# Long-convolution filters: plain float32 products in the taps' transform, without the split into high and low parts

## The chip, the cores and the metric

The kernel runs on one core of one Trainium2 chip. The metric is device time in microseconds (us) of one execution. Three runs of the kernel before took 3436.69, 3432.41 and 3435.01 us, median 3435.01 us. The engines are named as the profile names them: PE is TensorE's matmul side and PEld its weight load, DVE is VectorE, ACT is ScalarE, POOL is GpSimd, SP issues the DMAs.

## The reference, cut to what matters

The program is two blocks of a network on 512 tokens of 1024 channels (batch 1), with a context of 256 tokens beside them in the second block. The change lies in one function of the second block, the implicit filters of its long convolutions, which are computed once for n = 256 (context) and once for n = 512 (tokens):

```python
def hyena_filter_freqs(n, w1, b1, w2, b2, w3, freq):
    ...
    hid = jnp.sin(freq[0] * (z @ w1.astype(f32) + b1.astype(f32)))
    hid = jnp.sin(freq[1] * (hid @ w2.astype(f32) + b2.astype(f32)))
    h = (hid @ w3.astype(f32)).reshape(n, 2, HYENA_ORDER, D_B)
    deltas = jnp.abs(jnp.linspace(MIN_DECAY, MAX_DECAY, D_B, dtype=f32))
    h = h * jnp.exp(-t[:, :, None, None] * deltas)
    h_circ = jnp.concatenate(
        [h[:, 0], jnp.zeros((1, HYENA_ORDER, D_B), f32), h[:0:-1, 1]], axis=0)
    h_circ = h_circ / jnp.sum(jnp.abs(h_circ), axis=0, keepdims=True)
    return jnp.fft.rfft(h_circ, axis=0)
```

A small network of sines gives the taps h of two halves (forward and backward in time), two orders and 1024 channels; they are windowed, normalised by the sum of their magnitudes, and transformed over time. Everything is float32.

## The kernel before, in words

Most products of the kernel are made from split operands: `split` (L106) writes H, the operand in 12 significant bits, on ACT (L110), and L, what is left, on DVE (L113); `mm3` (L140) then adds three products, H.H, H.L and L.H (L144 to L146), in a PSUM bank. A few products are made with plain float32 operands and no split, among them the context's own long convolution (L1306, L1333); L1306 makes 32 products of 128 by 128 by 256 (two orders, four channel groups, two frequency tiles, two halves).

The filters come from `hyena_filter` (L1082), one generator for n = 256 and one for n = 512. Its three parts:

- `features` (L1102): the two sine layers, into HL.
- `matrices` (L1130): two constant matrices, cosine and sine, [time, frequency]; they are loaded in pieces and split into H and L by `split` (six pieces over both lengths).
- `groups` (L1208): eight groups of 256 channels. `taps(g)` (L1144) makes for each time tile of 128 (nt = 2 or 4 tiles) a bank with two products (L1160, L1161), the windowed taps `sd` on DVE (L1164; 512 columns, the sum of the two halves beside their difference), a correction of row 0 in the first tile (L1168, L1169), the magnitudes on ACT (L1172) and their sums (L1174, L1177 on DVE, L1178 on POOL), and then the split of `sd`: H on ACT (L1180), L in two halves (L1183), one on DVE and one on POOL. `transform(g, SD, i, nm)` (L1193) makes for each frequency tile (hk = 1 or 2) one bank with the products of the even times in columns 0 to 255 and of the odd times in 256 to 511, each by `mm3`; ACT copies the whole bank to `ae` (L1202), DVE adds its halves (L1204), POOL subtracts them (L1205), and SP sends the result to DRAM (L1206).

Over both lengths there are 48 time tiles, 48 transform banks and 160 products of 128 by 128 by 256, which are 480 matmuls as `mm3` makes them. The bank tag `h_pt` has two buffers, `h_ps` two, `h_sd` two, the split taps four each of H and L, `h_ae` two, `h_hg` three.

`second_block` runs the filters in turns with `gmlp` of the context (first half of its mixer), a step of each at a time. [...] What comes after the filters is the norm of the 512 tokens, and `hyena` of the context in turns with `gmlp` of the tokens; these use the SBUF and the PSUM banks that the filters' pools give back.

Of the kernel before, what the change touches and what calls it, by code (L numbers as in the profile page):

```python
# [17 lines left out]
ALU = mybir.AluOpType  # L18
# [11 lines left out]
class Ctx:  # L30
    """The program's pools and constants."""
# [26 lines left out]
class Scope:  # L58
    """Pools that live for some of the program."""
# [46 lines left out]
def split(k, H, L, src, act=True):  # L106
    """H = src in 12 significant bits, L = what is left."""
    nc = k.nc
    if act:
        nc.scalar.activation(out=H, in_=src, func=AF.Copy)  # L110
    else:
        nc.vector.tensor_copy(out=H, in_=src)
    nc.vector.tensor_tensor(out=L, in0=src, in1=f(H), op=ALU.subtract)  # L113


def wload(k, ap, n, nk, raws=None):
    """ap: DRAM [128, nk*n] -> list over k of (H, L) access patterns [128, n]; raws: the words, if they are loaded."""
    nc = k.nc
    per = max(1, 1024 // n)
    out = []  # L120
    for k0 in range(0, nk, per):
        kk = min(per, nk - k0)
        if raws:
            raw = raws[k0 // per]
        else:
            raw = k.raw.tile([P, kk * n], F32, tag="raw", name="raw", bufs=k.raw_bufs)
            nc.sync.dma_start(out=raw, in_=ap[:, k0 * n:(k0 + kk) * n])
        H = k.wsp.tile([P, kk * n], F32R, tag="wh", name="wh", bufs=k.w_bufs)
        L = k.wsp.tile([P, kk * n], F32R, tag="wl", name="wl", bufs=k.w_bufs)
        split(k, H, L, raw)  # L130
        for t in range(kk):
            out.append((H[:, t * n:(t + 1) * n], L[:, t * n:(t + 1) * n]))
    return out
# [6 lines left out]
def mm3(k, out, terms):  # L140
    """out = sum over terms of (sh+sl).T @ (mh+ml), but for sl.T @ ml, which lies below float32's last bit."""
    n = len(terms)
    for i, ((sh, sl), (mh, ml)) in enumerate(terms):
        k.nc.tensor.matmul(out=out, lhsT=sh, rhs=mh, start=(i == 0), stop=False)  # L144
        k.nc.tensor.matmul(out=out, lhsT=sh, rhs=ml, start=False, stop=False)  # L145
        k.nc.tensor.matmul(out=out, lhsT=sl, rhs=mh, start=False, stop=(i == n - 1))  # L146


class Tr:
    """A transposed activation, [channel, token], in pieces of some channel tiles, high and low parts."""  # L150
# [19 lines left out]
def power(k, ss, w, mult, add, tag="st"):  # L170
    """(ss*mult + add) ** -0.5"""
    nc = k.nc
    a = st(k, w, tag)
    nc.vector.tensor_scalar(out=a, in0=ss, scalar1=mult, scalar2=add, op0=ALU.mult, op1=ALU.add)  # L174
    r = st(k, w, tag)
    nc.gpsimd.tensor_tensor(out=r, in0=a, in1=k.neghalf[:, 0:w], op=ALU.pow)  # L176
    return r


def row_rstd(k, xm, j):  # L180
    """1 / rms of each row; j is room for the squares."""
    ss = st(k, 1)
    k.nc.scalar.activation(out=j, in_=xm, func=AF.Square, accum_out=ss)
    return power(k, ss, 1, 1.0 / 1024, EPS)


def norm_T(k, xm, g, T, m, b=None):
    """rms norm of the token tile xm [128, 1024], times g, plus b (both [128, 8], by channel), into T at tokens m."""
# [38 lines left out]
def tok_mm(k, T, m, w, off=0, ks=None):  # L227
    """The token tile m of T.T @ W in a bank."""
# [6 lines left out]
def add_out(*a, **kw):  # L235
    """x += gate * (T.T @ W), W in column groups of 512."""
    for _ in add_out_steps(*a, **kw):
        pass


def add_out_steps(k, W, T, nk=8, x=None, nt=4, gate=None, after=None, order=None, off=0, lag=2):
    """add_out, a step at a time."""
# [24 lines left out]
def turns(*gens):  # L267
    """Steps of several generators in turn; a pair (generator, n) takes n steps at a time."""
# [14 lines left out]
class Late(list):  # L283
    """Work that waits for other engines, put off by a step."""
# [7 lines left out]
def grp(w, cols):  # L292
    """[K, N] -> [128, (K/128) * len(cols)], the columns of one group, tile by tile of K."""
# [129 lines left out]
def hyena_consts(n, A):  # L423
    """Constants of a sequence length: positional features, decay windows, and the transforms."""
# [33 lines left out]
def a_tables(k, j):  # L458
    """Rotation tables with the gains folded in: [128, 4 token tiles, (q, k), 64]."""
# [18 lines left out]
def a_lambda(k, j, lam_init):  # L478
    """-(exp(q1.k1) - exp(q2.k2) + lambda_init) on every partition, [128, 1]."""
# [13 lines left out]
def layer_a(k, j, lam_init, T, after, w0=None):  # L493
# [51 lines left out]
    def attn(u, i):  # L545
        """A step for each head; the products that wait for a step's other engines come a step later."""
# [80 lines left out]
def layer_b(k, T, after, side):  # L627
    """side: a generator of other work, whose 96 steps are spread over the layer."""
# [24 lines left out]
    def conv(cs, us):  # L653
        """The sums of the taps of two channel tiles, in turn."""
# [20 lines left out]
    def turn(cs, accs):  # L675
        """The sums to token order."""
# [69 lines left out]
def layer_c(k, T, after):  # L746
# [25 lines left out]
    def rope(out, x, t, m, nh):  # L772
        """out = rotated x, both [128, nh, 64]; the gain is in the tables."""
# [120 lines left out]
    def attn(u, i):  # L894
        """A step for each head; the products that wait for a step's other engines come a step later."""
# [73 lines left out]
def mod_setup(k, pool):  # L969
    """silu of both conditions as 32 stationary columns, of which two are used: [128, 8, 32]."""  # L970
# [13 lines left out]
def mod_layers(k, pool, psum, raw_bufs):  # L984
    """The modulation vectors of both layers as columns, [128, 48 (section, channel tile), (c, c_ctx)], in 96 steps."""
# [36 lines left out]
def mod_affine(k, pool, l, which, s, tag):  # L1022
    """Gain and shift by channel of modulate(): g*(1+scale) [128, 8] and shift."""
# [9 lines left out]
def mod_gate(k, pool, l, which, s, tag):  # L1033
    """The gate as a row on every partition, [128, 1024]."""
# [12 lines left out]
def once(make):  # L1047
    """make(), at the first call."""
# [13 lines left out]
def sine(k, out, arg, t):  # L1062
    """out = sin(arg), by way of the remainder of arg by 2 pi; arg is destroyed, t is room."""
# [9 lines left out]
def hyena_filters(k, ns, pool, psum, out):  # L1073
    """The filters of several lengths, a step at a time."""
# [7 lines left out]
def hyena_filter(k, n, pool, psum, out, j):  # L1082
    """The spectra of both orders to DRAM, as (Hr, G) by order and channel group, and 1/(sum|h| 2n) by channel, into
    out[n]; three parts, a step at a time each. The filters' halves are held as their sum and difference, the larger
    magnitude of which is the sum of the halves' magnitudes."""
# [16 lines left out]
    def features():  # L1102
# [12 lines left out]
        h = room("h_sd", 2)[:, 0:n]  # L1115
# [8 lines left out]
        h = room("h_sd", 2)[:, 0:n]  # L1124
# [5 lines left out]
    def matrices():  # L1130
        for nm in ("c", "s"):
            H = pool.tile([P, nt, n // 2], F32R, tag=f"h_m{nm}h{n}", name="h_mh")
            L = pool.tile([P, nt, n // 2], F32R, tag=f"h_m{nm}l{n}", name="h_ml")
            mats[nm] = (H, L)
            for t in range(0, nt, 2):
                raw = room("h_raw", 2)[:, 0:n].rearrange("p (a b) -> p a b", a=2)
                nc.sync.dma_start(out=raw, in_=A[f"h_m{nm}_{n}"][:, t:t + 2])
                split(k, H[:, t:t + 2], L[:, t:t + 2], raw)
            yield
# [4 lines left out]
    def taps(g):  # L1144
        """The windowed sums and differences of a group of 256 channels, [time, channel], by time tile."""
# [11 lines left out]
        SD = [[], []]  # L1157
        for t in range(nt):
# [3 lines left out]
            sd = room("h_sd", 2)  # L1162
# [16 lines left out]
            H, L = (pool.tile([P, 512], F32R, tag=f"h_sd{c}", name="h_hl", bufs=4) for c in "hl")  # L1179
            nc.scalar.activation(out=H, in_=sd, func=AF.Copy)  # L1180
            for i, eng in enumerate((nc.vector, nc.gpsimd)):
                sl = slice(256 * i, 256 * i + 256)
                eng.tensor_tensor(out=L[:, sl], in0=sd[:, sl], in1=f(H[:, sl]), op=ALU.subtract)  # L1183
                SD[i].append((H[:, sl], L[:, sl]))
# [8 lines left out]
    def transform(g, SD, i, nm):  # L1193
        MH, ML = mats[nm]
        for kt in range(hk):
            p = bank("h_pt")
            sl = slice(kt * P, (kt + 1) * P)
            for par in range(2):
                mm3(k, p[:, 256 * par:256 * par + 256],
                    [((MH[:, t, sl], ML[:, t, sl]), SD[i][t]) for t in range(par * nt // 2, (par + 1) * nt // 2)])  # L1200
            ae = room("h_ae", 2)
            nc.scalar.activation(out=ae, in_=p, func=AF.Copy)  # L1202
            hg = pool.tile([P, 2, 256], F32, tag="h_hg", name="h_hg", bufs=3)
            nc.vector.tensor_tensor(out=hg[:, 0], in0=ae[:, 0:256], in1=ae[:, 256:512], op=ALU.add)  # L1204
            nc.gpsimd.tensor_tensor(out=hg[:, 1], in0=ae[:, 0:256], in1=ae[:, 256:512], op=ALU.subtract)  # L1205
# [20 lines left out]
def hyena_tables(k, n, pool, exact):  # L1226
    """The half-sample transforms, forward [t, k] and back [k, t], of both symmetries."""
# [21 lines left out]
def conv_input(k, pool, psum, n, spec, o, cg, z, exact):  # L1249
    """The spectrum of the filter, and z's halves folded and turned to [time, channel]."""  # L1250
# [32 lines left out]
def long_conv(k, pool, psum, n, tabs, D, o, cg, z, ready, exact, skip, out, then=None):  # L1283
    """z (*) filter + skip z, by channel tile; z and the result, out: lists of two [128 channels, n] each; ready: of
    conv_input; then: to be done when that has been used. A step at a time."""
# [72 lines left out]
class Stream:  # L1358
    """A sequence of the second block: n tokens, the residual xs, the transposed input T and the gate row."""
# [11 lines left out]
def gmlp(k, S, G, psum):  # L1371
    """xs += gate * (first half of the mixer), a step at a time."""
# [53 lines left out]
def hyena(k, S, pool, psum, spec, D, exact, after=None):  # L1426
    """xs += gate * (second half of the mixer), a step at a time."""
# [56 lines left out]
def ffn(k, l, streams):  # L1484
    """streams: (T, n, xs, gate, after) each; xs += gate() * swiglu(T)."""
# [34 lines left out]
def layer_attn(k, T, Tc, gate, after, opool):  # L1520
# [89 lines left out]
    def attn(g, i):  # L1610
        """The products that wait for a head's other engines come a head later."""
# [236 lines left out]
```

## Time and profile before

| | us |
|---|---|
| median of three runs | 3435.01 |
| lowest and highest | 3432.41, 3436.69 |
| span of the profiled execution, first to last instruction | 3436.0 |
| PE busy over the span | 3187.3 (93%) |
| DVE busy over the span | 2062.6 (60%) |
| POOL busy over the span | 868.9 (25%) |

For the profiled execution the page gives the span and no other time. Busy time of PE is modelled: matmuls are pipelined, so that one which starts behind another shows a longer duration than the distance to the next start. Stretches are given in us from the span's start; the filters lie between about 1344 and 1588.

### The profile page before, as it was taken

To read this page: it belongs to the slowest core of one execution; us is meant where nothing else is said; L and a number is where in the kernel's file an instruction comes from. 1 tells how busy PE (TensorE), PEld (TensorE's weight loads), DVE (VectorE), ACT (ScalarE), POOL (GpSimd) and SP (SyncE) were. 2 spreads that over 40 slices of the span, in tenths; PEclk is the share of its full clock that TensorE was granted. 3 is DMA by queue.
4 is the path that set the end of the run, shared out by engine and by line. 5 is a ranking of instruction groups with operands and counts; after the bars stand their busy time and mean duration, and the time that the engine had idled before them with its cause. 6 is when DMAs were issued, how large, how long until landed. Compare 5 with 4: busy or idle time off the path is not lost.

```text
span 3436.0 us, 43198 instructions
## 1 busy us (share of the span) xinstructions
PE 3187.3 (93%) x16196; PEld 2499.9 (73%) x16196; DVE 2062.6 (60%) x3794; ACT 1311.9 (38%) x2532; POOL 868.9 (25%) x790
## 2 busy tenths in 40 slices
PE   8999987889999999789999899799999999989998
PEld 6666533478676667668887788588888877778887
DVE  5665799555655666898667677733333265544334
ACT  5444534344444445555333333421222243442222
POOL 1110466101111111784433234212211120012111
PEclk9999998999999999799999999899999999999999
DMA  3112565521021114454333422111112110022222
GB/s 124 50 50 72 192 191 183 191 73 60 28 74 62 62 50 131 146 157 140 121 122 118 125 84 89 53 62 62 62 63 72 63 56 25 25 80 92 95 96 86
DMA packets 109073, 316.35 MB, mean 92 GB/s; under 512 B 11774, under 2 KB 29727, under 8 KB 108864
## 3 DMA queue, kind: packets, MB, share of 16 engines
q1 hardware_dynamic: 108432, 313.17, 28.5%
q8 instruction: 127, 2.08, 0.3%
q14 instruction: 82, 0.67, 0.1%
q10 hardware_dynamic: 432, 0.43, 0.0%
HBM read 297.83 MB, written 15.73 MB: 91 GB/s over the span
## 4 chain that ended last, share of the span: by engine, by line
PE 64%; DVE 18%; ACT 5%; POOL 5%; issue 4%; DMA 3%; POOLq 0%; DVEq 0%; ACTq 0%; SPq 0%
PE mm L144 16%; PE mm L146 16%; PE mm L145 16%; DVE b_a L665 4%; DVE wl L113 3%; PE sc L591 2%; POOL st L176 2%; PE sc L1655 1%; PE fc L144 1%; PE fc L145 1%; PE fc L146 1%; ACT wh L110 1%; PE o L1630 1%; PE o L558 1%; PE pq L1333 1%
## 5 line engine op out<-in xcount | busy, mean ns | idle before, releaser
L113 DVE TENSOR_TENSOR wl<-raw,wh 128x1024 fp32r<-128x1024 f32 (+2 forms) x400 | 506.7, 1270 | 338.5 <-ACT wh L110 333.6
L110 ACT ACTIVATE wh<-raw 128x1024 fp32r<-128x1024 f32 (+2 forms) x400 | 420.4, 1054 | 583.8 <-PE mm L146 303.3
L144 PE MATMUL mm<-wh,Th 128*128 128x512 f32 (+3 forms) x1200 | 459.4, 383 | 16.4 <-ACT Th L110 4.1
L144 PE MATMUL mm<-Th,wh 128*128 128x512 f32 x1152 | 458.8, 399 | 15.1 <-ACT s L693 7.8
L146 PE MATMUL mm<-Th,wl 128*128 128x512 f32 x1152 | 455.5, 396 | 9.7 <-DVE wl L113 9.6
L145 PE MATMUL mm<-wl,Th 128*128 128x512 f32 (+3 forms) x1200 | 452.6, 377 | 7.8 <-DVE wl L113 7.8
L145 PE MATMUL mm<-Tl,wh 128*128 128x512 f32 x1152 | 455.6, 396 | 0.0
L146 PE MATMUL mm<-wh,Tl 128*128 128x512 f32 (+3 forms) x1200 | 450.2, 376 | 1.3 <-DVE Tl L212 1.0
L176 POOL TENSOR_TENSOR st<-st,neghalf 128x1 f32<-128x1 f32 (+4 forms) x134 | 131.0, 977 | 739.3 <-DVE st L174 693.9
L1511 POOL TENSOR_TENSOR x<-s,x 128x512 f32<-128x512 f32 x88 | 120.8, 1378 | 704.3 <-DVE s L1510 704.1
L144 PEld LDWEIGHTS mm<-Th,wh 128*128 128x128 f32 x1152 | 219.4, 191 | 85.1 <-issue 24.3
L146 PEld LDWEIGHTS mm<-Th,wl 128*128 128x128 f32 x1152 | 218.4, 190 | 75.5 <-issue 18.4
L144 PEld LDWEIGHTS mm<-wh,Th 128*128 128x128 f32 x1200 | 229.9, 192 | 59.0 <-ACT Th L110 6.3
L145 PEld LDWEIGHTS mm<-Tl,wh 128*128 128x128 f32 x1152 | 219.0, 190 | 61.4 <-issue 18.4
L145 PEld LDWEIGHTS mm<-wl,Th 128*128 128x128 f32 x1200 | 230.1, 192 | 43.9 <-DVE wl L113 12.6
L146 PEld LDWEIGHTS mm<-wh,Tl 128*128 128x128 f32 x1200 | 229.3, 191 | 37.5 <-DVE Tl L212 3.3
L665 DVE SCALAR_TENSOR_TENSOR b_a<-b_u,b_cw,b_a 128x512 f32<-128x512 f32 x144 | 177.6, 1263 | 1.8
L670 POOL TENSOR_TENSOR b_p<-b_p,b_m 128x512 f32<-128x512 f32 x88 | 143.5, 1631 | 77.6 <-ACT b_m L668 63.2
L1510 DVE TENSOR_TENSOR s<-mm,gate 128x512 f32<-128x512 f32 x120 | 82.4, 690 | 125.4 <-PE mm L146 125.0
L144 PE MATMUL mm<-wh,f_g0h 128*128 128x512 f32 x352 | 137.9, 392 | 3.2 <-DVE s L1510 3.0
L145 PE MATMUL mm<-wl,f_g0h 128*128 128x512 f32 x352 | 137.1, 389 | 0.0
L146 PE MATMUL mm<-wh,f_g0l 128*128 128x512 f32 x352 | 136.7, 391 | 0.0
(431 smaller groups left out, 6644.1 us busy)
## 6 DMA issues: line engine op xcount, KB each, us to landing
m_raw<-in_mod_w_dram SPq DMA_DIRECT2D x96, 512.0 KB, 4.4
raw<-in_f_gu_dram SPq DMA_DIRECT2D x88, 512.0 KB, 3.8
raw<-in_e_in_dram SPq DMA_DIRECT2D x80, 512.0 KB, 4.4
raw<-in_a_in_dram SPq DMA_DIRECT2D x60, 512.0 KB, 4.2
raw<-in_f_dn_dram SPq DMA_DIRECT2D x44, 512.0 KB, 3.8
raw<-in_e_out_dram SPq DMA_DIRECT2D x32, 512.0 KB, 4.0
raw<-in_b_in_dram SPq DMA_DIRECT2D x24, 512.0 KB, 6.2
h_spec<-h_hg SPq DMA_DIRECT2D x48, 256.0 KB, 2.5
```

What stands on the lines that cost most here:

```text
L110: nc.scalar.activation(out=H, in_=src, func=AF.Copy)
L113: nc.vector.tensor_tensor(out=L, in0=src, in1=f(H), op=ALU.subtract)
L144: k.nc.tensor.matmul(out=out, lhsT=sh, rhs=mh, start=(i == 0), stop=False)
L145: k.nc.tensor.matmul(out=out, lhsT=sh, rhs=ml, start=False, stop=False)
L146: k.nc.tensor.matmul(out=out, lhsT=sl, rhs=mh, start=False, stop=(i == n - 1))
L176: nc.gpsimd.tensor_tensor(out=r, in0=a, in1=k.neghalf[:, 0:w], op=ALU.pow)
L558: nc.tensor.matmul(out=o[:, h * P:(h + 1) * P], lhsT=wT[:, b * P:(b + 1) * P], rhs=v[:, b, h * P:(h + 1) * P], start=(b == 0), stop=(b == i))
L591: nc.tensor.matmul(out=s[:, 0:n], lhsT=qT[64 * m:64 * m + 64, h, i * P:n], rhs=kT[64 * m:64 * m + 64, h, 0:n], start=True, stop=False)
L665: nc.vector.scalar_tensor_tensor(out=av, in0=uk, scalar=w, in1=av, op0=ALU.mult, op1=ALU.add)
L670: nc.gpsimd.tensor_tensor(out=ap, in0=ap, in1=q, op=ALU.add)
L1510: nc.vector.tensor_tensor(out=t, in0=y, in1=gate[:, c * 512:(c + 1) * 512], op=ALU.mult)
L1511: (nc.vector if part == 5 and c == 1 else nc.gpsimd).tensor_tensor(out=x_, in0=t, in1=x_, op=ALU.add)
```

## The change

`matrices` loads the two matrices whole, as float32, and splits nothing. `taps` no longer splits `sd`; the float32 tile itself goes to the transform, and its tag has ten buffers in place of two (the eight buffers of H and L are gone). `transform` makes one plain float32 product where `mm3` made three. ACT then copies only the first half of the bank, and both the sum and the difference are made on DVE, each from that copy and the second half of the bank where it lies in PSUM; POOL has no part in it. The rest of the diff takes out docstrings.

```diff
@@ matrices
         for nm in ("c", "s"):
-            H = pool.tile([P, nt, n // 2], F32R, tag=f"h_m{nm}h{n}", name="h_mh")
-            L = pool.tile([P, nt, n // 2], F32R, tag=f"h_m{nm}l{n}", name="h_ml")
-            mats[nm] = (H, L)
-            for t in range(0, nt, 2):
-                raw = room("h_raw", 2)[:, 0:n].rearrange("p (a b) -> p a b", a=2)
-                nc.sync.dma_start(out=raw, in_=A[f"h_m{nm}_{n}"][:, t:t + 2])
-                split(k, H[:, t:t + 2], L[:, t:t + 2], raw)
+            mats[nm] = pool.tile([P, nt, n // 2], F32, tag=f"h_m{nm}{n}", name="h_m")
+            nc.sync.dma_start(out=mats[nm], in_=A[f"h_m{nm}_{n}"])
             yield
@@ taps (the tag h_sd likewise in features)
-            sd = room("h_sd", 2)
+            sd = room("h_sd", 10)
...
-            H, L = (pool.tile([P, 512], F32R, tag=f"h_sd{c}", name="h_hl", bufs=4) for c in "hl")
-            nc.scalar.activation(out=H, in_=sd, func=AF.Copy)
-            for i, eng in enumerate((nc.vector, nc.gpsimd)):
-                sl = slice(256 * i, 256 * i + 256)
-                eng.tensor_tensor(out=L[:, sl], in0=sd[:, sl], in1=f(H[:, sl]), op=ALU.subtract)
-                SD[i].append((H[:, sl], L[:, sl]))
+            SD.append(sd)
@@ transform
             for par in range(2):
-                mm3(k, p[:, 256 * par:256 * par + 256],
-                    [((MH[:, t, sl], ML[:, t, sl]), SD[i][t]) for t in range(par * nt // 2, (par + 1) * nt // 2)])
-            ae = room("h_ae", 2)
-            nc.scalar.activation(out=ae, in_=p, func=AF.Copy)
+                for t in range(par * nt // 2, (par + 1) * nt // 2):
+                    nc.tensor.matmul(out=p[:, 256 * par:256 * par + 256], lhsT=mats[nm][:, t, kt * P:(kt + 1) * P],
+                                     rhs=SD[t][:, 256 * i:256 * i + 256], start=(t == par * nt // 2),
+                                     stop=(t == (par + 1) * nt // 2 - 1))
+            ae = room("h_ae", 2)[:, 0:256]
+            nc.scalar.activation(out=ae, in_=p[:, 0:256], func=AF.Copy)
             hg = pool.tile([P, 2, 256], F32, tag="h_hg", name="h_hg", bufs=3)
-            nc.vector.tensor_tensor(out=hg[:, 0], in0=ae[:, 0:256], in1=ae[:, 256:512], op=ALU.add)
-            nc.gpsimd.tensor_tensor(out=hg[:, 1], in0=ae[:, 0:256], in1=ae[:, 256:512], op=ALU.subtract)
+            nc.vector.tensor_tensor(out=hg[:, 0], in0=ae, in1=p[:, 256:512], op=ALU.add)
+            nc.vector.tensor_tensor(out=hg[:, 1], in0=ae, in1=p[:, 256:512], op=ALU.subtract)
             nc.sync.dma_start(out=dst[g // 4, g % 4, :, kt:nk:hk, i], in_=hg)
```

## Rows read from the trace of the kernel before

**Rows 1.** The page, busy tenths of PE and DVE in 40 equal slices.
```profile
PE   8999987889999999789999899799999999989998
...
DVE  5665799555655666898667677733333265544334
```

**Rows 2.** Windows: stretch, length, busy us (instructions) of PE, PEld, DVE, ACT, POOL; clock; DMA.
```profile
1344.00:1376.00 32.00, 29.58 (x199) 26.76 (x200) 27.69 (x48) 22.05 (x33) 7.75 (x8) 0.88 0.60 194
1376.00:1440.00 64.00, 44.85 (x210) 37.71 (x209) 53.39 (x91) 32.43 (x58) 47.86 (x47) 0.68 0.42 129
1440.00:1588.00 148.00, 121.32 (x750) 104.14 (x749) 140.21 (x221) 83.04 (x143) 118.22 (x123) 0.97 0.50 156
1344.00:1588.00 244.00, 195.76 (x1154) 168.61 (x1155) 221.29 (x359) 137.51 (x233) 173.84 (x177) 0.88 0.49 154
1588.00:1640.00 52.00, 50.42 (x404) 48.27 (x402) 37.78 (x75) 31.30 (x62) 11.25 (x17) 1.00 0.46 151
```

**Rows 3.** Waits, 1350 to 1590: who waited for whom, us in total, times, longest us.
```profile
PE h_ps L1160 <- DVE h_sd L1164: 17.3, 10, 2.6
...
PE h_pt L145 <- DVE h_hl L1183: 6.6, 11, 1.3
...
ACT h_ae L1202 <- DVE h_hg L1204: 6.4, 3, 3.7
...
PE h_pt L145 <- POOL h_hl L1183: 5.9, 7, 2.6
```

**Rows 4.** Groups of DVE by form, 1344 to 1590: count, busy us, mean ns, idle before.
```profile
L113 DVE TENSOR_TENSOR wl<-raw,wh 128x1024 fp32r<-128x1024 f32 x25 | 34.5, 1379 | 0.7 <-ACT wh L110 0.5
L1204 DVE TENSOR_TENSOR h_hg<-h_ae 128x256 f32<-128x256 f32 x48 | 34.1, 723 | 5.7 <-ACT h_ae L1202 5.5
...
L1183 DVE TENSOR_TENSOR h_hl<-h_sd,h_hl 128x256 fp32r<-128x256 f32 x48 | 30.6, 649 | 0.5
L1177 DVE TENSOR_TENSOR h_mx<-h_ab 128x256 f32<-128x256 f32 x32 | 21.5, 673 | 0.0
...
L113 DVE TENSOR_TENSOR h_ml<-h_raw,h_mh 128x512 fp32r<-128x512 f32 x4 | 3.3, 817 | 0.4 <-ACT h_mh L110 0.4
```

**Rows 5.** Groups of POOL by form, 1344 to 1590.
```profile
L1205 POOL TENSOR_TENSOR h_hg<-h_ae 128x256 f32<-128x256 f32 x48 | 47.0, 989 | 14.0 <-ACT h_ae L1202 6.9 <-DMA h_spec<-h_hg 2.9 <-ACT h_ab L1172 2.9
L1183 POOL TENSOR_TENSOR h_hl<-h_sd,h_hl 128x256 fp32r<-128x256 f32 x48 | 47.0, 990 | 15.5 <-ACT h_hl L1180 15.1
```

**Rows 6.** Single lines, DVE: ns min/median/max, first and last start us, form.
```profile
L1164 DVE TENSOR_TENSOR h_sd<-h_ps,h_win x48: 670/678/693, 1373.5 to 1578.2; 128x512 f32<-128x512 f32 x48
L1204 DVE TENSOR_TENSOR h_hg<-h_ae x48: 404/937/1514, 1384.6 to 1587.2; 128x256 f32<-128x256 f32 x48
L1316 DVE TENSOR_TENSOR y_b<-uv,y_hg x16: 408/415/421, 1612.8 to 1869.2; 128x256 f32<-128x256 f32 x16
L113 DVE TENSOR_TENSOR wl<-raw,wh x36: 1215/1225/1226, 2409.5 to 2690.7; 128x1024 fp32r<-128x1024 f32 x36
```

**Rows 7.** Busy time in 1344 to 1588 of the instructions on h_pt alone (PE, PEld, ACT).
```profile
1344.00:1588.00 244.00, 82.53 (x480) 71.82 (x480) 27.54 (x48) 0.88 0.49 154
```

**Rows 8.** Timeline of PE: start us, us, matmul; split products at two clocks.
```profile
1522.30 0.28 PE L144 MATMUL h_pt<-h_hl,h_mh 128*128 128x256 f32 x1
1522.42 0.28 PE L145 MATMUL h_pt<-h_hl,h_mh 128*128 128x256 f32 x1
...
1557.12 0.41 PE L144 MATMUL h_pt<-h_hl,h_mh 128*128 128x256 f32 x1
...
1557.33 0.41 PE L145 MATMUL h_pt<-h_hl,h_mh 128*128 128x256 f32 x1
```

**Rows 9.** Plain float32 products of the context's convolution: timeline of two, then the line.
```profile
1609.04 0.59 PE L1306 MATMUL uv<-y_z,h_f 128*128 128x256 f32 x2
...
L1306 PE MATMUL uv<-y_z,h_f x64: 377/378/483, 1609.0 to 1867.2; 128*128 128x256 f32 x64
```

**Rows 10.** DMA issues, 1344 to 1588: the cosine matrix, count, KB each, median us to landing.
```profile
h_raw<-in_h_mc_dram SPq DMA_DIRECT2D x2, 256.0 KB, 4.1
```

More of the change, by code (lines that the diff above doesn't have):

```diff
@@ L30 @@
 class Ctx:
+    pass
 def setup(es, tc, A, index):
@@ L1114, in features @@
         t = room(*(("h_ab", 1), ("h_ae", 2))[j])[:, 0:n]
-        h = room("h_sd", 2)[:, 0:n]
+        h = room("h_sd", 10)[:, 0:n]
         nc.vector.tensor_scalar(out=a[0:64], in0=p[0:64, 0:n], scalar1=sc[0:64, 0:1], scalar2=sc[0:64, 1:2],
@@ L1123, in features @@
                                 op1=ALU.mult)
-        h = room("h_sd", 2)[:, 0:n]
+        h = room("h_sd", 10)[:, 0:n]
         sine(k, h, a, t)
@@ L1156, in taps @@
         acc = pool.tile([P, 256], F32, tag="h_acc", name="h_acc", bufs=3)
-        SD = [[], []]
+        SD = []
         for t in range(nt):
@@ L1193, in transform @@
     def transform(g, SD, i, nm):
-        MH, ML = mats[nm]
         for kt in range(hk):
             p = bank("h_pt")
-            sl = slice(kt * P, (kt + 1) * P)
             for par in range(2):
-                mm3(k, p[:, 256 * par:256 * par + 256],
-                    [((MH[:, t, sl], ML[:, t, sl]), SD[i][t]) for t in range(par * nt // 2, (par + 1) * nt // 2)])
-            ae = room("h_ae", 2)
-            nc.scalar.activation(out=ae, in_=p, func=AF.Copy)
+                for t in range(par * nt // 2, (par + 1) * nt // 2):
[4 more added lines that the diff above has]
+            nc.scalar.activation(out=ae, in_=p[:, 0:256], func=AF.Copy)
             hg = pool.tile([P, 2, 256], F32, tag="h_hg", name="h_hg", bufs=3)
-            nc.vector.tensor_tensor(out=hg[:, 0], in0=ae[:, 0:256], in1=ae[:, 256:512], op=ALU.add)
-            nc.gpsimd.tensor_tensor(out=hg[:, 1], in0=ae[:, 0:256], in1=ae[:, 256:512], op=ALU.subtract)
+            nc.vector.tensor_tensor(out=hg[:, 0], in0=ae, in1=p[:, 256:512], op=ALU.add)
+            nc.vector.tensor_tensor(out=hg[:, 1], in0=ae, in1=p[:, 256:512], op=ALU.subtract)
             nc.sync.dma_start(out=dst[g // 4, g % 4, :, kt:nk:hk, i], in_=hg)
```

## The prediction

> **What bounds the kernel now.** I read the page's slices first, then windows over the stage of the filters, then waits and groups inside it. Over the whole span TensorE is the bound; the reader is to see in the slices that there is one stage, slices 16 to 18, where PE falls to 7 and 8 tenths while VectorE stands at 8 and 9 [rows 1]. The windows place it: from 1344 to 1588 us VectorE is busy 221.3 of 244 us (91%), TensorE 195.8 (80%), GpSimd 173.8 (71%), ScalarE 137.5. Behind it, from 1588 to 1640, TensorE is at 97% and VectorE at 73% [rows 2]. So time saved in the stage moves everything behind it forward at full price, since the next stage waits for the filters' memory and is then bound by TensorE, which has the same work as before. In the stage TensorE's waits are mostly for VectorE's products: 17.3 us for the windowed taps, 6.6 us for L's half on VectorE, 5.9 us for GpSimd's [rows 3].
>
> One more thing is to be seen: L1204, both operands in SBUF, takes 404 ns at least but 937 ns in the median, whereas L1164, one operand in a bank and the other in SBUF, never leaves 670 to 693 ns in 48 instructions; L1316 with a bank operand stays in 408 to 421 ns [rows 6]. With GpSimd busy 71% of the stage, instructions of VectorE with two SBUF operands are slowed beside it, and those with one are not.
>
> **The change part by part.** All sums are for 1344 to 1588 in the profiled execution, whose span is 3436.0 us, 1.0 us above the median of the runs.
>
> *VectorE, removed:* 48 halves of L, 30.6 us; the splits of the matrices' four larger pieces, 3.3 us (two smaller ones left out); the 48 old sums, 34.1 us [rows 4]. *Added:* 48 sums and 48 differences with one operand in a bank. The form is not in this stage; the nearest row is L1316, the same size and operands, 415 ns [rows 6]: 96 x 0.415 = 39.8 us. From below it is bounded by L1204's fastest, 404 ns (38.8 us), from above by L1204's median, 937 ns (90.0 us). I take 39.8, the nearest form. *Relieved:* GpSimd loses L1183 and L1205, 47.0 us each [rows 5], so 94.0 of its 173.8 us, 54%. The instructions with two SBUF operands that stay then meet it less often: L1177, 32 at a mean of 673 where the same size can take 404, is 8.6 us too long, and the weight split, 25 at 1379 against 1225 in a later stretch, 3.9 us [rows 4, 6]. 54% of 12.5 is 6.7 us, an estimate with bounds 0 and 12.5. Sum: 221.3 - 30.6 - 3.3 - 34.1 + 39.8 - 6.7 = 186.4 us.
>
> [...] L1316 differs from L1204's fastest by 11 ns [rows 6]. [...]
>
> *TensorE:* 480 split matmuls go. In the timeline they start 0.12 us apart, and 0.21 us apart where the clock is low [rows 8]: 480 x 0.12 = 57.6 us. A plain product leaves two records: L1306 has 64 records for 32 products. Two of them cover 0.59 us and one takes 0.378, so the second starts 0.21 us behind the first [rows 9]: 160 products x 2 x 0.21 = 67.2 us. That is 9.6 us more. Bounds: if the records of a product came as close as the split ones (0.12), 320 x 0.12 - 57.6 = -19.2 us; if they did not overlap at all (0.378) against the present busy time of 82.5 us [rows 7, 9], 121.0 - 82.5 = +38.5 us. I take +9.6, the same form seen in a full stretch.
>
> [...] TensorE's need: 195.8 + 9.6 - 7.2 = 198.2 us.
>
> *Cost nothing:* ScalarE loses 48 splits and half of each copy; it had 106 us free [rows 2]. The matrices move the same bytes in four DMAs in place of six; the pieces for n = 512 come as one, so its first use may be later by a transfer, which TensorE's other work in the head (29.6 of 32 us busy [rows 2]) hides; without that cover one transfer, 4.1 us [rows 10]. Ten buffers of h_sd take the room of the ten there were (two, four, four), and the next group's taps no longer stop two tiles ahead; that takes away waits already counted as idle time.
>
> *A wait is added:* a transform bank comes free only when VectorE has made its second read, no longer when ScalarE has copied it. Queued ahead of that read are weight splits and taps; behind the bank, TensorE's queue with everything in it. It is priced below as the slower rival.
>
> *The sum:* the larger need moves from VectorE (221.3) to TensorE (198.2), with VectorE close (186.4). An engine that bounds reaches 91% here and 97% in the next stage [rows 2]. I take 92%, near the row of this stage, since two engines are close and each waits for the other: 198.2 / 0.92 = 215.4 us instead of 244.0, so -28.6 us; 3436.0 - 28.6 = 3407.4, less the 1.0 us between the profile and the median: 3406.4.
>
> **The rivals.**
>
> [...]
>
> *TensorE binds with the waits left.* No clock is won and it reaches 88%: 205.4 / 0.88 = 233.4, -10.6, so 3424. For it: TensorE had 80%, not all of whose gaps are VectorE's, and the two banks of the transform. Against: all the named waits in rows 3 lose their cause or are shortened.
>
> *VectorE stays the bound, no gain.* The difference is moved to the busiest engine. If the 96 bank reads took the mean of the SBUF form, 723 ns, they would cost 69.4 us against the 68.0 removed, and without relief VectorE's need is 222.7, at 91% 244.7 us: 3436. Against: the 48 even durations of L1164. [...]
>
> *Slower: the bank is held by VectorE's queue.* There are two banks, filled in 2 x 0.42 = 0.84 us (16 times, n = 256) or 1.68 us (32 times, n = 512). A bank's release takes ScalarE's copy, 27.54 / 48 = 0.57 us [rows 7], one weight split queued ahead on VectorE, 1.38 [rows 4], and two reads, 0.83: 2.8 us. What the fill of the other bank doesn't cover is 16 x 1.96 + 32 x 1.12 = 67 us at most. With half of it on TensorE's path, 34 us against the 28.6 gained, the time is 3440; with all of it 3473. It decides from 0.6 us per bank. Against: today's chain, two banks and two copies that wait for VectorE and GpSimd, shows 6.4 us in three waits [rows 3], and TensorE's queue has other matmuls between the banks.
>
> **How the numbers follow.** Forecast 0.50, own range 3395 to 3416 (the clock's bounds and 90 to 95%); tight packing 0.20; waits left 0.18; no gain 0.06; slower 0.06. Of this kernel 0.2%, some 7 us, is what a measurement can tell from no change. Faster by more than that, under 3428: the first two and nearly all of the third, 0.86. Within: 0.08; slower: 0.06. The range 3384 to 3427 takes in the forecast, most of tight packing and most of the waits left, some 0.8.
>
> **What would show it.** Right: the filters end some 29 us earlier and the stretches behind have their old lengths; VectorE's two reads of a transform bank take 0.41 to 0.42 us each whatever GpSimd does; the transform's records start 0.21 us apart, 320 of them; GpSimd falls to some 80 us in the stage, VectorE to some 186; the clock around the filters for n = 256 rises above 0.68. Wrong: TensorE waiting for VectorE's reads before a transform bank (the held bank), VectorE again above 210 us (no gain), a longer distance than 0.21 us, or the stages behind growing by what the filters save, which my sum takes to be nothing.

## The result and the profile after

The changed kernel takes 3399.34 us (median of four runs, 3393.06 to 3401.0) against 3434.22 us of the kernel before (median of four): a ratio of 0.9891, 95% interval [0.9879, 0.9903]. Run again beside the variants below it gave 0.9879 [0.9864, 0.9894], 3395.39 against 3438.99 us. The two agree within their intervals; 35 to 44 us are gained, where 28.6 were forecast. The profiled execution is the fastest of its four, 3393.06 us with a span of 3391.3 us, so its 44.7 us less of span lie at the upper end. The time of this execution is 1.8 us above its span; if that holds for the kernel before, its profile, with a span of 3436.0, shows an execution above the highest of its four runs, which adds to this.

Where the time went is read from two lines of each trace: the first matmul of the filters (L1112) and the last sending of a spectrum (L1206 before, L1196 after). First the kernel before: count, ns min/median/max, first and last start in us.

```profile
L1112 PE MATMUL h_ps<-h_raw,h_w x4: 376/742/1112, 1332.3 to 1336.1; 33*64 33x256 f32 x2, 33*64 33x512 f32 x2
...
L1206 SPq DMA_DIRECT2D h_spec<-h_hg x48: 512/518/597, 1385.6 to 1588.2; - x48
```

The same two lines of the kernel after:

```profile
L1112 PE MATMUL h_ps<-h_raw,h_w x4: 376/508/640, 1329.4 to 1332.5; 33*64 33x256 f32 x2, 33*64 33x512 f32 x2
...
L1196 SPq DMA_DIRECT2D h_spec<-h_hg x48: 512/518/736, 1376.8 to 1542.7; - x48
```

From the first to the last it was 255.9 us and is 213.3, 42.6 less. Behind it there were 3436.0 - 1588.2 = 1847.8 us and there are 3391.3 - 1542.7 = 1848.6. Everything was gained inside the filters' stage and nothing given back behind it; the remaining 2.9 us lie ahead of the stage, whose start moved between 1328 and 1335 us over all the traces of this study.

The windows after, as in [rows 2] (length, then busy us of PE, PEld, DVE, ACT, POOL, the clock, DMA):

```profile
1376.00:1440.00 64.00, 54.99 (x268) 45.16 (x267) 60.16 (x123) 28.06 (x53) 30.24 (x31) 0.89 0.59 187
1440.00:1543.00 103.00, 95.47 (x491) 81.63 (x490) 86.46 (x178) 45.80 (x88) 37.33 (x41) 1.00 0.54 176
1344.00:1543.00 199.00, 179.11 (x964) 152.91 (x963) 174.39 (x348) 95.23 (x171) 74.35 (x80) 0.96 0.57 183
1543.00:1595.00 52.00, 50.80 (x401) 48.16 (x401) 38.61 (x74) 33.28 (x62) 10.86 (x15) 1.00 0.43 136
```

The reader is to see two engines that end almost level: TensorE at 179.1 of 199 us (90%, it was 80%), VectorE at 174.4 (88%, it was 91%). GpSimd fell from 173.8 to 74.4. The granted clock of the stage rose from 0.88 to 0.96. The stretch behind is as before.

The groups of VectorE after, as in [rows 4], for 1344 to 1543:

```profile
L113 DVE TENSOR_TENSOR wl<-raw,wh 128x1024 fp32r<-128x1024 f32 x22 | 29.1, 1324 | 2.9 <-ACT wh L110 2.8
L1195 DVE TENSOR_TENSOR h_hg<-h_ae,h_pt 128x256 f32<-128x256 f32 x48 | 19.7, 410 | 0.0
L1194 DVE TENSOR_TENSOR h_hg<-h_ae,h_pt 128x256 f32<-128x256 f32 x48 | 19.6, 409 | 5.5 <-ACT h_ae L1192 4.7 <-ACT h_ab L1167 0.7
L1172 DVE TENSOR_TENSOR h_mx<-h_ab 128x256 f32<-128x256 f32 x32 | 17.4, 544 | 3.1 <-ACT h_ab L1167 2.8
```

The 96 bank reads take 39.3 us at 410 ns. L1172 (L1177 before), whose own code did not change, went from 673 to 544 ns beside the less busy GpSimd.

TensorE's waits after, as in [rows 3]:

```profile
PE h_pt L1188 <- DVE h_hg L1195: 5.2, 4, 1.5
...
PE h_ps L1155 <- DVE h_sd L1159: 2.4, 4, 1.0
```

The 17.3 us of waits for the windowed taps are 2.4, those for the split taps are gone, and the wait that the change adds, a bank held by VectorE's second read, costs 5.2 us in four times.

The transform on TensorE: seven records of the timeline (start us, us), and the busy time of all that touches h_pt, as in [rows 7] (here PE, PEld, DVE, ACT):

```profile
1539.71 1.67 PE L1188 MATMUL h_pt<-h_sd,h_m 128*128 128x256 f32 x7
```

```profile
1344.00:1543.00 199.00, 80.32 (x320) 62.06 (x320) 36.54 (x96) 17.92 (x48) 0.96 0.57 183
```

Seven records in 1.67 us, the last some 0.38 long (the median of the 320 records is 379 ns), start (1.67 - 0.38) / 6 = 0.215 us apart.

### The profile page after: what moved, and what is told of

It reads as the page before. It is cut to its first block, busy times and chain, and to the rows that moved or that the text cites. A ratio compares the mean times of both kernels' runs of the same rounds, so it can differ in the third digit from the quotient of the medians.

```text
span 3391.3 us, 42613 instructions
## 1 busy us (share of the span) xinstructions
PE 3176.5 (94%) x16036; PEld 2490.1 (73%) x16036; DVE 2017.7 (59%) x3788; ACT 1274.6 (38%) x2478; POOL 770.3 (23%) x694
## 4 chain that ended last, share of the span: by engine, by line
PE 65%; DVE 17%; ACT 5%; issue 5%; POOL 4%; DMA 2%; POOLq 0%; SPq 0%; ACTq 0%; DVEq 0%
PE mm L144 16%; PE mm L145 16%; PE mm L146 16%; DVE b_a L665 4%; DVE wl L113 3%; PE sc L591 2%; POOL st L176 2%; PE h_pt L1188 1%; PE sc L1645 1%; PE fc L144 1%; PE fc L146 1%; PE fc L145 1%; ACT wh L110 1%; PE o L1620 1%; PE o L558 1%
```

## The experiments

Each variant was measured together with the kernel before, in three groups. Between the groups, times are compared by the ratio to the kernel before, whose median was 3434 to 3439 us; 0.001 is 3.4 us. Letters such as A or C stand for the theories in the expectation above the result.

**The change without its last part.** The edit, against the changed kernel:

```diff
-            ae = room("h_ae", 2)[:, 0:256]
-            nc.scalar.activation(out=ae, in_=p[:, 0:256], func=AF.Copy)
+            ae = room("h_ae", 2)
+            nc.scalar.activation(out=ae, in_=p, func=AF.Copy)
...
-            nc.vector.tensor_tensor(out=hg[:, 0], in0=ae, in1=p[:, 256:512], op=ALU.add)
-            nc.vector.tensor_tensor(out=hg[:, 1], in0=ae, in1=p[:, 256:512], op=ALU.subtract)
+            nc.vector.tensor_tensor(out=hg[:, 0], in0=ae[:, 0:256], in1=ae[:, 256:512], op=ALU.add)
+            nc.gpsimd.tensor_tensor(out=hg[:, 1], in0=ae[:, 0:256], in1=ae[:, 256:512], op=ALU.subtract)
```

> The change without its last part: ScalarE copies the whole bank again, VectorE adds the halves from SBUF, GpSimd subtracts them; plain products and no split stay. Theory A (after the change TensorE has the larger need, VectorE is a close second): GpSimd gets 48 instructions of about 0.95 us back (+46 us), VectorE loses 39 us of bank reads and gets 48 sums of 0.5 to 0.7 us (24 to 34 us) and somewhat slower neighbours, so its need stays about the same: 3394 to 3408 us, against 3399 of the whole change. Rival B (VectorE still binds, so that taking the difference off it helps): 10 to 20 us faster than the whole change, 3380 to 3390. Rival C (the bank reads on VectorE and the freed GpSimd are where the gain comes from): most of the gain is lost, 3420 or more.

Measured 3410.45 us, 0.9919 [0.9905, 0.9932], 15 us behind the changed kernel measured beside it (3395.39, 0.9879). A's range is missed by 2 us at the top; B forecast a gain over the whole change, and C the loss of most of the gain: neither came. Its window, its DVE group of the sums, and TensorE's wait for the taps:

```profile
1344.00:1560.00 216.00, 188.05 (x964) 158.23 (x965) 179.23 (x299) 105.14 (x173) 123.92 (x128) 0.93 0.52 167
...
L1194 DVE TENSOR_TENSOR h_hg<-h_ae 128x256 f32<-128x256 f32 x48 | 29.9, 625 | 8.0 <-ACT h_ae L1192 7.6
...
PE h_ps L1155 <- DVE h_sd L1159: 10.9, 10, 3.8
```

VectorE makes 48 instructions fewer and is still busy 5 us longer, its sums at 625 ns beside a GpSimd of 124 us, and TensorE waits 10.9 us for taps where it waited 2.4.

**The last part alone,** on the kernel before (the same lines, the other way; the splits and three products stay).

> The kernel before with the last part of the change alone: sum and difference on VectorE from the bank, with ScalarE copying half; the splits and the three products of each term stay. VectorE: 34.1 us of sums go, 39.5 come; GpSimd loses 47 us, which relieves VectorE's instructions with two SBUF operands by some 5 to 8 us. Theory A (the gain comes from the removed splits): 3425 to 3437 us, at most a quarter of the gain. Rival C (it comes from freeing GpSimd): 3405 to 3418. Rival D (the bank held by VectorE's queue costs): slower than before, 3440 or more.

Measured 3426.75 us, 0.9969 [0.9958, 0.9981]: 12 us faster than before. A's range holds, C and D are out. Its window:

```profile
1344.00:1579.00 235.00, 198.19 (x1152) 170.21 (x1152) 213.08 (x405) 123.81 (x229) 121.88 (x129) 0.87 0.49 155
```

VectorE's busy time fell from 221.3 to 213.1 us although it makes 48 instructions more, and the stage became shorter with it, at 91% in both. The reads cost 5 us more than the sums did. Counted group by group over the two windows, instructions that are in both got 5.7 us shorter beside the less busy GpSimd, as expected (L1183 and L1177 got 2.2 us longer, the others together 8 us shorter); 3.4 us are work that now lies outside the window, and the rest is no group's (records overlap, so the groups add up to more than the busy time: 242.8 against 221.3 us in the stage of the kernel before). 12 us here and the 28 us that the run above keeps of the gain add up to 41 of the 44 of the whole, measured together.

**The same two operations on VectorE, but from SBUF.**

```diff
-            nc.vector.tensor_tensor(out=hg[:, 0], in0=ae, in1=p[:, 256:512], op=ALU.add)
-            nc.vector.tensor_tensor(out=hg[:, 1], in0=ae, in1=p[:, 256:512], op=ALU.subtract)
+            nc.vector.tensor_tensor(out=hg[:, 0], in0=ae[:, 0:256], in1=ae[:, 256:512], op=ALU.add)
+            nc.vector.tensor_tensor(out=hg[:, 1], in0=ae[:, 0:256], in1=ae[:, 256:512], op=ALU.subtract)
```

> The whole change, but ScalarE copies the whole bank and VectorE makes sum and difference from the copy in SBUF, so that the bank is free after the copy. VectorE's 96 instructions then have two SBUF operands: with GpSimd busy some 37% of the stage, 0.5 to 0.6 us each instead of 0.41, 9 to 18 us more; ScalarE 10 us more. Theory A: 3402 to 3412 us, as VectorE becomes the larger need. Rival D (holding the bank costs TensorE more than its 5 us of visible waits): faster than the whole change, 3390 to 3396.

Measured 3409.47 us, 0.9918 [0.9904, 0.9931]: A. Its window and its two groups:

```profile
1350.00:1561.00 211.00, 183.67 (x962) 154.81 (x962) 185.35 (x348) 104.16 (x171) 79.69 (x80) 0.95 0.54 172
...
L1194 DVE TENSOR_TENSOR h_hg<-h_ae 128x256 f32<-128x256 f32 x48 | 27.2, 566 | 5.9 <-ACT h_ae L1192 5.7
L1195 DVE TENSOR_TENSOR h_hg<-h_ae 128x256 f32<-128x256 f32 x48 | 26.0, 542 | 0.0
```

53.2 us instead of 39.3, at an equal count. Moving the difference to VectorE gained nothing by itself: from SBUF it is no better than on GpSimd (3410.45). What gained is that one operand comes from the bank. Freeing the bank earlier did not pay for that: TensorE's waits for a transform bank fell from 5.2 to 2.3 us only. The run changes both at once, so it does not price the held bank by itself.

**The changed kernel again,** as their measure.

> The changed kernel itself once more, on the same chip as the three variants, as their measure and for a second profile of it: 3393 to 3401 us as in its runs so far. Its profiled execution was the fastest of its four (3393 against 3398 to 3401); theory: the extra 5 to 8 us of the others lie in one place, which a second profile may show if it falls on a slower one; rival: they are spread over the span.

3395.39 us (3392.95 to 3398.02). Its profile again shows an execution near the lower end (span 3391.6), so where the longer ones spend their extra time stays open.

**More work for VectorE.**

```diff
             nc.vector.tensor_tensor(out=hg[:, 1], in0=ae, in1=p[:, 256:512], op=ALU.subtract)
+            nc.vector.tensor_tensor(out=hg[:, 1], in0=ae, in1=p[:, 256:512], op=ALU.subtract)
```

> The changed kernel with the difference made twice on VectorE: 48 more bank reads of 0.41 us, 19.7 us of VectorE's time in the filters' stage, on no other engine. The changed kernel takes 3395 to 3399 us. Theory A (TensorE has the larger need, 90% busy, VectorE second at 88%): part of it is taken up by VectorE's 25 us of idle time, +5 to +12 us, 3401 to 3410. Theory B (VectorE still binds, as the 14 us that reads from SBUF cost one for one suggest): +17 to +22 us, 3413 to 3420.

3407.16 us, 0.9921 [0.9908, 0.9933]: by the ratios 10 us behind the changed kernel's first measurement and 14 behind its second, for 19.7 us of work. By its time A, but more than half of the work is seen.

**More work for TensorE.**

```diff
-            for par in range(2):
+            for par in (0, 1) * (2 if nm == "c" else 1):
```

> The changed kernel with the products of the cosine transform issued twice into the same bank (the second chain starts afresh, so that the sum is the same): 80 products, 160 records at 0.21 us, 33.6 us more of TensorE, on no other engine. Theory A (TensorE binds): +25 to +34 us, 3422 to 3432. Theory B (VectorE binds, TensorE has 20 us of idle time): +5 to +15 us, 3402 to 3413. If both are dear one for one, the two queues wait for each other in turn and neither has slack: A and B both hold in part.

3421.59 us, 0.9967 [0.9954, 0.9979]: 26 to 30 us for 33.6. That is 0.4 us below A's range and 9 above B's. The windows of these two runs, VectorE's first:

```profile
1344.00:1556.00 212.00, 189.30 (x995) 159.52 (x994) 188.91 (x400) 99.25 (x179) 71.38 (x81) 0.94 0.55 174
```

```profile
1344.00:1573.00 229.00, 213.81 (x1121) 184.59 (x1122) 178.41 (x348) 96.53 (x174) 77.01 (x81) 0.96 0.50 161
```

With more for VectorE both engines end at 89%; with more for TensorE it is at 93% and VectorE at 78%. So after the change added work costs about 0.8 to 0.9 of itself on TensorE and 0.5 to 0.7 on VectorE: TensorE is the larger need, and VectorE has little room beside it.

**Six buffers of h_sd in place of ten.**

```diff
-            sd = room("h_sd", 10)
+            sd = room("h_sd", 6)
```

> The changed kernel with six buffers of h_sd in place of ten, so that the next group's taps for n = 512 can run only two tiles ahead of a transform that still needs its four. Theory R (room to run ahead took away the 17 us of TensorE's waits for the windowed taps): 8 to 15 us slower, 3404 to 3412. Rival (these waits came from VectorE's lateness, the room is of no account): within 4 us of the changed kernel, 3394 to 3402.

The tag in `features` is edited likewise. 3394.68 us, 0.9890 [0.9876, 0.9903]: the rival. Ten buffers in place of six are of no account: with six, TensorE waits 3.0 us for the windowed taps, with ten 2.4. That the 17 us before were VectorE's lateness fits this; fewer than six were not run.

**One more piece from VectorE to GpSimd.**

```diff
-        split(k, WH, WL, ws)
+        nc.scalar.activation(out=WH, in_=ws, func=AF.Copy)
+        nc.gpsimd.tensor_tensor(out=WL, in0=ws, in1=f(WH), op=ALU.subtract)
```

> The changed kernel with one more piece of work moved from VectorE to GpSimd, which is now 37% busy in the stage: the low part of the taps' last weights (16 subtractions of 128x512, 14 us on VectorE at 0.88 us each; on GpSimd some 1.4 to 1.7 us each, 22 to 27 us). Theory B (VectorE binds, and what counts is its need): 5 to 10 us faster, 3387 to 3393, since GpSimd's longer reads slow VectorE's two-operand instructions a little. Theory A (TensorE binds): within 4 us, 3394 to 3402. If contention eats more than it frees: slower, 3403 or more.

3402.51 us, 0.9907 [0.9892, 0.9922]: not faster, and by the ratios 5 to 10 us slower, though the intervals overlap. The time falls between A's range and the last of the three; B is out. Its window:

```profile
1344.00:1552.00 208.00, 182.08 (x968) 155.97 (x967) 170.20 (x333) 94.47 (x173) 98.53 (x95) 0.94 0.55 177
```

GpSimd got 24 us more. Within the window 13.4 us of subtractions left VectorE, but its busy time fell by 4 only: group by group, the instructions that stayed got 7.5 us longer beside the busier GpSimd.

**Three split products with no subtraction on VectorE or GpSimd.** The matrices are split as before, and the taps' high part, made on ScalarE, stands where the low part stood.

```diff
-            SD.append(sd)
+            H = pool.tile([P, 512], F32R, tag="h_sdh", name="h_hl", bufs=8)
+            nc.scalar.activation(out=H, in_=sd, func=AF.Copy)
+            SD.append(H)
...
```

Left out of this diff: the matrices' six pieces as in the kernel before, `mm3` in the transform, and two buffers of h_sd in place of ten.

> The changed kernel with three split products in place of each plain one: the matrices are split again (six pieces), ScalarE makes the high part of the taps (48 copies of 0.62 us), and that high part stands where the low part stood, so that neither VectorE nor GpSimd subtracts (the low part of the taps is left out of the result). TensorE: 480 x 0.12 instead of 320 x 0.21 us, 9.6 us less; VectorE 4.5 us more, ScalarE 31 us more. By the slopes seen (0.7 for TensorE's time, 0.5 for VectorE's): some 4 us faster than the changed kernel's 3395 to 3399, 3389 to 3396. Rival (a product that waits for ScalarE's copy of its operand comes later, and this latency outweighs the 9.6 us): 3400 to 3410.

3398.57 us, 0.9886 [0.9872, 0.9899]: the same as the changed kernel, between the two expectations. The busy time of all that touches h_pt, as in [rows 7]:

```profile
1344.00:1553.00 209.00, 73.18 (x480) 67.19 (x480) 36.12 (x96) 17.93 (x48) 0.91 0.58 184
```

On TensorE the transform is busy 73.2 us where it was 80.3, so 7.1 of the 9.6 us are saved there. They are not seen in the time: VectorE is busy 10 us longer (184.2 us in 209, against 174.4), and TensorE waits 4.5 us, in six times, for ScalarE's copies. In the time of the kernel the form of the product is neither a gain nor a loss that this run can tell; some 4 us, as expected, would be at its limit.

**The taps' split made, but read by nothing.**

```diff
+            H, L = (pool.tile([P, 512], F32R, tag=f"h_sd{c}", name="h_hl", bufs=2) for c in "hl")
+            nc.scalar.activation(out=H, in_=sd, func=AF.Copy)
+            for i, eng in enumerate((nc.vector, nc.gpsimd)):
+                sl = slice(256 * i, 256 * i + 256)
+                eng.tensor_tensor(out=L[:, sl], in0=sd[:, sl], in1=f(H[:, sl]), op=ALU.subtract)
             SD.append(sd)
```

> The changed kernel with the split of the taps still made on ScalarE, VectorE and GpSimd, but read by nothing: 28 us of ScalarE, 30 us of VectorE and 47 us of GpSimd come back, and no wait of TensorE on them. Theory S (the slopes: VectorE's 30 us and some 5 us of contention at 0.5): 15 to 20 us slower than the changed kernel, 3411 to 3419. Theory B (VectorE's need counts one for one as soon as it is the largest): VectorE needs 174 + 35 = 209 us and TensorE 179, so 28 to 35 us slower, 3424 to 3433. Rival L (what the split cost was the latency it put between taps and products, not the engines' time): within 8 us of the changed kernel, 3396 to 3406.

3427.05 us, 0.9966 [0.9952, 0.9979]: B, 26 to 30 us of the gain are gone again with work whose results no engine reads. Its window and VectorE's group of the unread split:

```profile
1344.00:1574.00 230.00, 193.05 (x994) 159.48 (x993) 211.24 (x399) 121.82 (x223) 122.45 (x129) 0.94 0.50 161
...
L1178 DVE TENSOR_TENSOR h_hl<-h_sd,h_hl 128x256 fp32r<-128x256 f32 x48 | 33.0, 702 | 0.7 <-ACT h_hl L1175 0.2
```

VectorE is back at 211 of 230 us, 92%, as before the change. The kernel before with the last part alone has nearly the same busy times of VectorE and GpSimd (213.1 and 121.9 us) and the same time (0.9969), although there three products wait for the split that here nothing reads. So what the split cost is the engines' time; the wait between taps and products adds nothing that these two runs can tell. TensorE's records of the transform are the same 320 as in the changed kernel, and they show 86.0 us of busy time in place of 80.3, with 15.2 us of idle time in front of them in place of 7.6 (the granted clock of the stage is 0.94 in place of 0.96, which the busy time holds too):

```profile
L1193 PE MATMUL h_pt<-h_sd,h_m 128*128 128x256 f32 x320 | 86.0, 411 | 15.2 <-DVE h_hg L1200 9.5 <-ACT h_hl L1175 2.5 <-ACT h_ae L1197 1.3
```

**Two small pieces from VectorE to ScalarE** (the halving of row 0, in the changed kernel 16 instructions of 418 ns in the mean, and the scaling of the sums, 16 of some 150 ns).

```diff
-                nc.vector.tensor_scalar(out=s3[0:1], in0=both.unsqueeze(1).to_broadcast([1, 2, 256]), scalar1=0.5,
-                                        scalar2=None, op0=ALU.mult)
+                nc.scalar.activation(out=s3[0:1], in_=both.unsqueeze(1).to_broadcast([1, 2, 256]), func=AF.Copy,
+                                     scale=0.5)
...
-        nc.vector.tensor_scalar(out=D[:, 2 * g:2 * g + 2], in0=p[:, 0:2], scalar1=2.0 * n, scalar2=None, op0=ALU.mult)
+        nc.scalar.activation(out=D[:, 2 * g:2 * g + 2], in_=p[:, 0:2], func=AF.Copy, scale=2.0 * n)
```

> [...] VectorE 9 us less, ScalarE some 13 us more. By the slope 0.5: 3 to 5 us faster than the changed kernel, 3390 to 3395. Rival (ScalarE comes later to the magnitudes and copies, which VectorE then waits for): same or slower, 3396 to 3404.

3396.85 us, 0.9884 [0.9871, 0.9898]: the rival, no change that can be measured, though VectorE has 9 us less to do: it is busy 165.5 of the 199 us from 1344 to 1543, where it was 174.4, and ScalarE 104.1, where it was 95.2. No variant beats the change.

## Why the prediction came out right, and where it was too small

- *VectorE binds the stage, and its removed work is the gain:* right. The splits that nothing reads show it from the other side: they take 26 to 30 us back, with VectorE at 92% again.
- *Bank reads at 415 ns:* right, 409 and 410 ns in the two groups after, and with them the last part alone is 12 us faster than before. These means lie 5 to 6 ns above the 404 of the fastest SBUF read [rows 6].
- *Relief from GpSimd, 6.7 us:* too small, and its upper bound of 12.5 too. Group by group over the two windows, the instructions that are in both got 13.7 us shorter. L1172 gave 32 x (673 - 544) = 4.1 us; the prediction had summed two groups only, and others with two SBUF operands were slowed as well. So was L1169 before (L1164 after), with one operand, in SBUF: 575 ns in the mean, 418 after. That instructions with one SBUF operand are not slowed was therefore shown for those with the other operand in a bank, and not beyond them. VectorE's need was put at 186.4 us and is 174.4; besides the relief, some 5 us of its other work now lie outside the window.
- *TensorE's records 0.21 us apart, 9.6 us more:* the distance is right (0.215). Against the kernel before the cost does not show: the transform is busy 80.3 us after 82.5. The same 480 split matmuls are busy 73.2 us in the run with three products, so the 82.5 held some 9 us of waits and lower clock that the sum, at 57.6 us, left out. Against that run 7.1 us of the cost show in TensorE's busy time, and none in the kernel's time.
- *TensorE's need, 198.2 us at 92%:* this is the term that was mis-sized. It is 179.1 us at 90%, and the stage 199 us where 215.4 were forecast (the 92% was 2 points too high, which makes up some 4 us the other way). Of the 19 us, 11.8 lie in the transform's own records (2.2 us less than before, not 9.6 more) and 7.3 in TensorE's other matmuls. What follows divides the same 19 us by cause, as an estimate. The 7.2 us in the sum were my estimate of half the clock's return in one stretch, 1376 to 1440; no run shows that term by itself, nor the clock's bounds behind the range. What the traces show in its place: in windows of 1 us over the stage the clock is 0.50 in 51 of 244 before and in 11 of 199 after, 1.00 in 179 and 181, and between the two in the rest; the stretch went from 0.68 to 0.89, but the whole stage from 0.88 to 0.96, that is from some 2 x 0.12 x 244 = 59 us at 0.50 to 2 x 0.04 x 199 = 16 us. At some 80% busy, and with half of the time at 0.50 taken as lost (the split products start 0.21 us apart there, 0.12 at 1.00), half of the 43 us between is 17 us, 10 more than I took. Another 4 us are 30 matmuls of the other stream (964 - 320 against 1154 - 480 in the windows, 0.12 us apart), which now lie outside the window. The last 5 us I put down, without a run of its own, to busy time that was no need: the transform's same records show 86.0 us instead of 80.3 in the run with the unread splits, with twice the waits and a slightly lower clock, which that run does not separate.
- *TensorE the larger need, VectorE close:* right, by the two runs with added work.
- *The held bank:* 5.2 us of waits, some 0.1 us per bank, far from the rival's point of decision of 0.6.
- *The difference on the busiest engine:* moving it from VectorE to GpSimd was the slower way here, by 10 to 15 us. The run that moved the weights' low part to GpSimd, by the ratios 5 to 10 us slower, agrees with that.
- *Nothing given back behind the stage:* right, 1847.8 and 1848.6 us.

## What to carry to other kernels

Before moving work off VectorE to GpSimd, see whether an operand can stay in the PSUM bank: the same operation took 410 ns from the bank, and 540 to 720 ns in the mean with two SBUF operands, with GpSimd busy 38 to 71% of the stage. What a stage gains by removed work is worked out from the engine that binds it, but the busy time of TensorE is no fixed need: here it fell from 195.8 to 179.1 us in the stage, part of it as the waits became fewer (for the windowed taps 17.3 us before, 2.4 after) and the granted clock rose (0.88 to 0.96). Where two engines were level here, 9 us taken off one of them did not show in the time.

## What was not expected of the hardware

A plain float32 product of 128 by 128 by 256 leaves two records 0.21 us apart and so takes 0.43 us, only some 20% more than the three split products at 0.12 us each that it replaces; with the splits counted it is the cheaper form in this stage, by the 26 to 30 us that the unread splits cost.

GpSimd's load shows on VectorE beyond the two groups that the prediction summed: with 94 us of GpSimd's work gone, the weight split (wl), one of these two, went from 1389 to 1324 ns in the stage (1344 to 1588 before, to 1543 after), and the two instructions of the one-row correction (L1168 and L1169 before) from 543 to 458 and from 575 to 418 ns. Of L1169 the median hardly moved (407 and 405 ns); its longest went from 1476 to 609 ns, so it is single instructions that are held up.
